# Running a depthwise convolution chunk by chunk on VectorE, with a mark for each chunk

## The chip, the cores and the metric

The kernel runs on one core of one Trainium2 chip. The metric is the device time of one execution in microseconds (us). The kernel before the change took 1326.59 us, the median of three runs (1323.63 to 1327.82).

The core's engines are named as the profile names them: PE is TensorE (matmuls; PEld is its weight load), DVE is VectorE, ACT is ScalarE, POOL is GpSimd, SP is SyncE, which issues every DMA here.

## The reference, cut to what matters

Two layers of a hybrid block work on 1024 latent tokens and 256 context tokens with 1024 channels. In each layer one input projection feeds three branches: a convolution module (256 channels), windowed attention with rotary tables (512) and a gated linear attention, GLA (256). Each branch is multiplied by a SiLU gate of its own, and one output projection joins them. The last layer needs no convolution, gate or output for the context tokens. The convolution module is:

```python
u = p['a_val'] * jax.nn.sigmoid(p['a_glu'])
u = lax.conv_general_dilated(u, conv_w[:, None, :], window_strides=(1,), padding=((15, 15),),
        feature_group_count=CONV_WIDTH) + conv_b          # depthwise, 31 taps along the tokens
mu, var = mean and variance of u over the 256 channels
u = (u - mu) * lax.rsqrt(var + NORM_EPS) * ln_w + ln_b
return jax.nn.silu(u) * jax.nn.silu(p['a_gate'])
```

## The kernel before, in words

**Layout.** Channels lie on the 128 partitions and tokens along the free dimension. The 256 convolution channels are two halves j = 0, 1. The 1280 tokens are three chunks, `CH`: chunk 0 is the 256 context tokens, chunks 1 and 2 are 512 latent tokens each. `col(t)` puts a gap of 15 columns between context and latents, so layer 0's whole token axis is 1280 + 15 = 1295 columns. The buffer `U[j]` holds the convolution's input with 15 zero columns at each end and in the gap. `mix` holds the three branches' results.

**The taps.** `conv_taps(l)` runs 31 taps for two halves on DVE. Each is one instruction over the whole axis, 1295 columns in layer 0 and 1024 in layer 1: the first tap is a `tensor_scalar` (input times weight plus bias), each other one a `scalar_tensor_tensor` that reads `U` shifted by s columns and the sum so far in `mix`, and writes the sum. These are the rows `mix<-U,small,mix` of the profile; both tensor inputs lie in SBUF. After the last one the mark `conv{l}` is set.

**What waits for the mark.** `ev_agate` takes the gate's projection out of PSUM (ACT `Tanh`, then one DVE instruction `U<-SM,ps`) and writes it over `U`, which the taps must have read by then. `conv_ln(l, c)` norms one chunk: PE transposes `mix` (rows `ps<-idr,mix`), DVE takes `BN_STATS`, PE transposes back, ACT and DVE apply swish and gate.

**What sets the order.** The program is a set of generators ("lanes") with priorities. A planner in the kernel keeps an estimated clock for each engine and asks the lanes, by priority, for their next instructions while it writes each engine's instructions in one fixed order. On the chip, each engine then runs its row in that order and waits where an operand is not ready. A lane can wait for a mark, a buffer, or an engine's estimated clock. The taps have the lowest priority of their stage (7) and are asked for with `yield self.idle("dve", 300)`: only when DVE's estimated queue reaches no more than 300 ns ahead. So they are put as filler between the DVE instructions of the other lanes.

**The stage.** `phase_a(l)` issues the projection groups in the order 0, 1 (the convolution's input), 10 (GLA values and decay), 8 (GLA queries and keys), 5, 3, 4 (attention keys, values, queries), 2 (the convolution's gate), 9, 6, 7 (other gates). `t_group` and `tok_group` issue the matmuls of a group. The taps start after group 1. The norm's lane is created behind the whole of group 2:

```python
            elif g == 2:
                yield from self.t_group(l, g, self.ev_agate(l), cx)
                def ln(): ...
                self.go(ln(), 3)
```

While the taps run, three other kinds of work go on. `gla_decay` makes the decays (`tensor_tensor_scan` on DVE). `gla_states` makes, for a chunk and a direction, e = last − b on DVE (`SM<-mix`), its exponential on ACT, its product with the keys on POOL (`SM<-SM,mix`), and PE's transposes of that product (`ps<-idr,SM`); later DVE adds up states (`mix<-mix,dec,ps`). `rope` turns keys and queries with five POOL instructions for each pair of token tiles: two `WR<-SM,SM`, one `SM<-SM,SM`, two `SM<-SM,WR`. `gla_out` makes the outputs of a token tile (`COPY_PREDICATED`, `TENSOR_REDUCE` and others on DVE). `split` cuts weights into two parts on ACT, DVE or POOL, whichever the planner thinks is free (`WS<-WR,WS`). `load_vz` issues the DMAs `SM<-vd`.

All instructions are issued through one helper, so every row has its line, L43.

Of the kernel before, what the change touches and what calls it, by code (L numbers as in the profile page):

```python
# [13 lines left out]
ALU = mybir.AluOpType  # L14
# [9 lines left out]
CH = [(0, 256), (256, 512), (768, 512)]  # L24


def col(t):
    return t if t < 256 else t + GAP
# [140 lines left out]
class Hybrid:  # L169
# [692 lines left out]
    def ev_agate(self, l):  # L862
        def ev(j, p, t0, n, c):
            nc = self.nc
            yield self.need("SM"), f"conv{l}"
            s = self.sm(512)
            t = s[:, 0:n]
            nc.scalar.activation(t, p, ACTF.Tanh, scale=0.5)
            yield
            nc.vector.scalar_tensor_tensor(self.U[j][:, col(t0):col(t0) + n], t, 1.0, p, op0=ALU.add, op1=ALU.mult)  # L870
            self.free(s)
            self.flag(f"ag{l}.{j}.{c}")
        return ev
# [71 lines left out]
                self.nc.vector.memset(self.U[j][:, a:a + n], 0.0)  # L945

    def conv_taps(self, l):
        nc = self.nc
        a, n = (0, 1295) if l == 0 else (271, 1024)
        for s in range(31):  # L950
            for j in range(2):
                yield self.idle("dve", 300)
                acc = self.mix(j, slice(a, a + n))
                src = self.U[j][:, a + s:a + s + n]
                if s == 0:
                    nc.vector.tensor_scalar(acc, src, self.p_conv_w(l, j, s), self.p_small(l, 62, j),
                                            op0=ALU.mult, op1=ALU.add)
                else:
                    nc.vector.scalar_tensor_tensor(acc, src, self.p_conv_w(l, j, s), acc, op0=ALU.mult, op1=ALU.add)
        self.flag(f"conv{l}")  # L960

    def conv_ln(self, l, c):
        nc = self.nc
# [620 lines left out]
    def phase_a(self, l):  # L1584
        cx = (0, 1) if l == 0 else ()
        self.units, self.pre, self.pcount = [], 0, 0
        self.conv_pad()
        if l:
            self.cap = dict(mm=2, tr=4, ac=2, md=2)
            self.evs = []  # L1590
        else:
            yield from self.t_start()
        first = (2, 0) if l == 0 else (1, 2, 0)
        for g in GROUPS[:-1]:
            if g == 10:
                self.cap = dict(mm=3, tr=2, ac=2, md=1)
                self.go(self.gla(l), 2)
                yield from self.vlr_group(l)
            elif g == 0 and l:
                yield from self.t_group(l, 0, self.ev_glu, cx, (1,), last=False)  # L1600
                yield from self.t_group(l, 1, self.ev_val, cx, (1,), last=False)
                yield from self.t_group(l, 0, self.ev_glu, cx, (2,))
            elif g == 0:
                yield from self.t_group(l, g, self.ev_glu, cx, first)
            elif g == 1:
                yield from self.t_group(l, g, self.ev_val, cx, (2,) if l else first)
                evs = tuple(self.evs)

                def conv():
                    yield evs  # L1610
                    yield from self.conv_taps(l)
                self.go(conv(), 7)
            elif g == 8:
                yield from self.t_group(l, g, self.ev_qk(l), (0, 1) if l == 0 else (1,))
                self.flag(f"qk{l}")
            elif g == 5:
                yield from self.tok_group(l, g, self.ev_qk_b(l, "kv", self.kd, 2))
            elif g in (3, 4):
                yield from self.tok_group(l, g, self.ev_qk_b(l, f"q{g - 3}", self.qd[:, :, (g - 3) * 256:(g - 2) * 256], 4), l == 0)
            elif g == 2:  # L1620
                yield from self.t_group(l, g, self.ev_agate(l), cx)

                def ln():
                    for c in range(1 if l else 0, 3):
                        yield from self.conv_ln(l, c)
                self.go(ln(), 3)
            elif g == 9:
                yield from self.t_group(l, g, self.ev_mgate(l, 6), cx)
            else:
                self.cap.update(mm=2, tr=CAPB[0], ac=CAPB[1])  # L1630
                self.cap["md"] = 0 if l else MDC
                if l:
                    self.flag(f"hcfree{l}")
                for n, (p, c) in enumerate(B_GATE):
                    if n == ATTN:
                        self.attn = self.go(self.attn_start(l), 1)
                    yield from self.t_group(l, p, self.ev_gate(l, 2 * p - 10), cx, order=(c,), last=all(x[0] != p for x in B_GATE[n + 1:]))
                    if n == MODG:
                        self.flag("mods")
                    if (p, c) == (7, 1):  # L1640
                        self.h1_keep()
                    if p == 7:
                        self.flag({0: f"hcfree{l}", 1: f"h1out{l}", 2: f"h2out{l}"}[c])
# [212 lines left out]
```

## Time and profile before

| | |
|---|---|
| median of three runs | 1326.59 us |
| the profiled execution | 1323.65 us, its span 1321.9 us |
| PE | 1254.0 us busy, 95% of the span |
| DVE | 838.4 us, 63% |
| ACT | 561.2 us, 42% |
| POOL | 452.9 us, 34% |
| mean granted PE clock | 0.991 |

The span is the time from the first to the last instruction. Rows of the timeline give start, duration, engine, operation, output tile <- input tiles, shape and a count; in brackets stands how long the engine had been idle before and what it waited for. Several instructions of a kind that follow each other are one row. PEclk is the granted clock of PE, 1.00 being full speed.

### The profile page before, as it was taken

To read this page: it belongs to the slowest core of one execution; us is meant where nothing else is said; L and a number is where in the kernel's file an instruction comes from. 1 tells how busy PE (TensorE), PEld (TensorE's weight loads), DVE (VectorE), ACT (ScalarE), POOL (GpSimd) and SP (SyncE) were. 2 spreads that over 40 slices of the span, in tenths; PEclk is the share of its full clock that TensorE was granted. 3 is DMA by queue.
4 is the path that set the end of the run, shared out by engine and by line. 5 is a ranking of instruction groups with operands and counts; after the bars stand their busy time and mean duration, and the time that the engine had idled before them with its cause. 6 is when DMAs were issued, how large, how long until landed. Compare 5 with 4: busy or idle time off the path is not lost.

```text
span 1321.9 us, 24553 instructions
## 1 busy us (share of the span) xinstructions
PE 1254.0 (95%) x9518; PEld 1066.9 (81%) x9518; DVE 838.4 (63%) x1571; ACT 561.2 (42%) x1280; POOL 452.9 (34%) x609
## 2 busy tenths in 40 slices
PE   6999988999999999899999899988999999999997
PEld 3668988898887777687899879977888888788897
DVE  5745897884364463465354676898954656766554
ACT  3721341235332565466541561441245246665531
POOL 1410045674122342444230241055571334344410
PEclk9999989999999999999999999999999999999999
DMA  9453113222014323342132541114231112231012
GB/s 330 151 154 105 48 39 85 70 69 85 25 33 131 112 77 100 96 129 89 49 113 88 156 164 57 49 41 108 71 91 37 55 46 81 73 93 50 33 65 81
DMA packets 113237, 116.49 MB, mean 88 GB/s; under 512 B 38464, under 2 KB 81760, under 8 KB 113120
## 3 DMA queue, kind: packets, MB, share of 16 engines
q1 hardware_dynamic: 113120, 114.92, 28.5%
q8 instruction: 75, 1.23, 0.4%
q14 instruction: 42, 0.34, 0.1%
HBM read 95.47 MB, written 19.42 MB: 87 GB/s over the span
## 4 chain that ended last, share of the span: by engine, by line
PE 69%; DVE 8%; POOL 6%; DMA 6%; issue 5%; ACT 4%; SPq 1%; POOLq 0%; DVEq 0%; ACTq 0%
PE ps L43 69%; POOL SM L43 4%; DVE SM L43 3%; ACT SM L43 2%; DVE mix L43 2%; DMA WR<-in_w_out_dram 2%; DVE H L43 2%; DMA WR<-in_w_mod_dram 2%; POOL WR L43 1%; DMA WR<-in_w_in_dram 1%; DVE WS L43 1%; SPq L43 1%; DMA HC<-in_w_mod_dram 1%; ACT H L43 1%; ACT L43 0%
## 5 line engine op out<-in xcount | busy, mean ns | idle before, releaser
L43 PE MATMUL ps<-H,WS 128*128 128x512 f32 x1344 | 339.7, 400 | 2.9 <-DVE stat L43 1.4
L43 PEld LDWEIGHTS ps<-H,WS 128*128 128x128 f32 x1344 | 244.3, 189 | 63.8 <-issue 12.2
L43 PE MATMUL ps<-WS,H 128*128 128x256 f32 x1744 | 254.8, 291 | 0.0
L43 PEld LDWEIGHTS ps<-WS,H 128*128 128x128 f32 x1744 | 230.4, 195 | 10.0 <-issue 9.5
L43 ACT ACTIVATE SM<-ps 128x512 f32<-128x512 f32 (+2 forms) x164 | 82.7, 509 | 343.6 <-PE ps L43 289.3
L43 DVE SCALAR_TENSOR_TENSOR mix<-U,small,mix 128x1295 f32<-128x1295 f32 (+1 forms) x120 | 180.9, 1549 | 0.0
L43 PE MATMUL ps<-idr,SM 128*128 128x128 f32 (+1 forms) x1076 | 150.5, 273 | 26.2 <-POOL SM L43 16.4
L43 PEld LDWEIGHTS ps<-idr,SM 128*128 128x128 f32 (+1 forms) x1076 | 120.0, 142 | 56.0 <-POOL SM L43 22.0
L43 DVE CUSTOM_DVE_ANT_0 SM<-ps,SM,small 128x640 f32<-128x640 f32 (+2 forms) x128 | 102.7, 813 | 60.1 <-PE ps L43 53.5
L43 ACT ACTIVATE SM<-SM,stat 128x641 f32<-128x641 f32 (+2 forms) x144 | 110.7, 769 | 69.5 <-DVE stat L43 47.2
L43 POOL TENSOR_TENSOR tir<-tir,mhalf 128x1 f32<-128x1 f32 (+2 forms) x55 | 47.3, 863 | 199.2 <-DVE tir L43 192.3
L43 POOL TENSOR_TENSOR SM<-SM,SM 128x128 fp32r<-128x128 f32 (+3 forms) x59 | 60.9, 1041 | 158.7 <-ACT SM L43 107.9
L43 PE MATMUL ps<-H,H 128*128 128x256 f32 x592 | 99.0, 287 | 3.7 <-DVE H L43 2.0
L43 ACT ACTIVATE H<-ps 128x512 f32<-128x512 f32 (+1 forms) x129 | 72.7, 596 | 65.2 <-PE ps L43 63.7
L43 POOL TENSOR_SCALAR SM<-SM,tir 128x640 f32<-128x640 f32 (+2 forms) x90 | 75.8, 855 | 44.3 <-DVE tir L43 29.7
L43 PEld LDWEIGHTS ps<-H,H 128*128 128x128 f32 x592 | 83.8, 189 | 5.5 <-DVE H L43 2.2
L43 ACT ACTIVATE SM<-SM 32x128 f32<-32x128 f32 (+3 forms) x194 | 70.3, 369 | 38.3 <-DVE SM L43 30.0
L43 PE MATMUL ps<-SM,SM 128*32 128x128 f32 (+4 forms) x764 | 79.0, 285 | 5.9 <-DMA SM<-vd 3.1
L43 PE MATMUL ps<-H 128*64 128x256 f32 x548 | 72.3, 388 | 0.7 <-ACT ps L43 0.3
L43 POOL TENSOR_TENSOR SM<-SM,WR 128x256 f32<-128x256 f32 (+2 forms) x60 | 61.8, 1036 | 20.0 <-DVE SM L43 13.8
L43 DVE TENSOR_TENSOR WS<-WR,WS 128x512 fp32r<-128x512 f32 x66 | 60.7, 932 | 5.2 <-ACT WS L43 3.6
L43 PEld LDWEIGHTS ps<-SM,SM 128*64 128x64 f32 (+2 forms) x764 | 45.4, 127 | 20.0 <-ACT SM L43 6.1
(151 smaller groups left out, 1989.8 us busy)
## 6 DMA issues: line engine op xcount, KB each, us to landing
WR<-in_w_in_dram SPq DMA_DIRECT2D x80, 256.0 KB, 3.7
WR<-in_w_mod_dram SPq DMA_DIRECT2D x64, 256.0 KB, 3.2
WR<-in_w_out_dram SPq DMA_DIRECT2D x32, 256.0 KB, 3.5
SM<-vd SPq DMA_DIRECT2D x116, 64.0 KB, 2.4
x<-SM SPq DMA_DIRECT2D x20, 256.0 KB, 2.5
SM<-x SPq DMA_DIRECT2D x20, 256.0 KB, 4.3
qd<-SM SPq DMA_DIRECT2D x18, 256.0 KB, 2.2
mix<-in_x_dram SPq DMA_DIRECT2D x8, 512.0 KB, 8.3
```

Source lines behind the costliest of these rows:

```text
L43: r = getattr(self._e, op)(*a, **k)
```

## The change

The convolution is run chunk by chunk: all 31 taps of both halves for chunk 0 (layer 0 only), then for chunk 1, then for chunk 2. A tap takes 256 or 512 columns in place of 1295 or 1024. After each chunk its mark `conv{l}.{c}` is set; the gate of that chunk waits for this mark alone, and so does the norm of that chunk.

```diff
     def ev_agate(self, l):
         def ev(j, p, t0, n, c):
             nc = self.nc
-            yield self.need("SM"), f"conv{l}"
+            yield self.need("SM"), f"conv{l}.{c}"
...
     def conv_taps(self, l):
-        nc = self.nc
-        a, n = (0, 1295) if l == 0 else (271, 1024)
-        for s in range(31):
-            for j in range(2):
-                yield self.idle("dve", 300)
-                acc = self.mix(j, slice(a, a + n))
-                src = self.U[j][:, a + s:a + s + n]
...
-        self.flag(f"conv{l}")
+
+        nc = self.nc
+        for c in range(1 if l else 0, 3):
+            a, n = col(CH[c][0]), CH[c][1]
+            for s in range(31):
+                for j in range(2):
+                    yield self.idle("dve", 300)
+                    acc = self.mix(j, slice(a, a + n))
+                    src = self.U[j][:, a + s:a + s + n]
...
+            self.flag(f"conv{l}.{c}")
...
                 def ln():
                     for c in range(1 if l else 0, 3):
+                        yield f"conv{l}.{c}"
                         yield from self.conv_ln(l, c)
```

The number of taps on DVE goes from 62 to 186 in layer 0 and from 62 to 124 in layer 1. The planner sees other estimated times and writes the rows in another order, within the two stages that hold the taps and for some way behind them.

First place: DVE in layer 0, about the second pair of GLA states. Before:

```order
L43 SCALAR_TENSOR_TENSOR mix_223_1356<-mix_223_1356,dec,ps_71 128x64 x4
L43 TENSOR_TENSOR SM_269_1764<-mix_223_1356 128x512
L43 SCALAR_TENSOR_TENSOR mix<-U,small,mix 128x1295 x6
L43 SCALAR_TENSOR_TENSOR mix_223_1356<-mix_223_1356,dec,ps_70 128x64 x8
L43 TENSOR_TENSOR SM_277_1930<-mix_223_1356 128x512
```

The same piece of DVE's row now:

```order
L43 SCALAR_TENSOR_TENSOR mix_223_1398<-mix_223_1398,dec,ps_71 128x64 x4
L43 TENSOR_TENSOR SM_269_1827<-mix_223_1398 128x512
L43 SCALAR_TENSOR_TENSOR mix<-U,small,mix 128x512 x14
L43 SCALAR_TENSOR_TENSOR mix_223_1398<-mix_223_1398,dec,ps_69 128x64 x8
L43 TENSOR_TENSOR SM_277_2000<-mix_223_1398 128x512
```

Six taps of 1295 columns have become fourteen of 512 at the same place; nothing else moved there. In layer 1 the piece that answers to it holds eight taps of 1024 columns before and fourteen of 512 now.

Second place: POOL in layer 0 at the same time, one rope and the product that PE's transposes wait for. Before:

```order
L43 TENSOR_TENSOR SM_267_1744<-SM_267_1744,mix 128x512
L43 TENSOR_TENSOR WR_273_1794<-SM_272_1793,SM_1_65 128x2x2x32 x2
L43 TENSOR_TENSOR SM_272_1793<-SM_272_1793,SM_1_65 128x2x128
L43 TENSOR_TENSOR SM_272_1793<-SM_272_1793,WR_273_1794 128x2x2x32 x2
L43 TENSOR_TENSOR SM_269_1764<-SM_269_1764,mix 128x512
```

Now:

```order
L43 TENSOR_TENSOR SM_267_1802<-SM_267_1802,mix 128x512
L43 TENSOR_TENSOR WR_273_1857<-SM_272_1856,SM_1_65 128x2x2x32 x2
L43 TENSOR_TENSOR SM_272_1856<-SM_272_1856,SM_1_65 128x2x128
L43 TENSOR_TENSOR SM_272_1856<-SM_272_1856,WR_273_1857 128x2x2x32 x2
L43 TENSOR_TENSOR SM_269_1827<-SM_269_1827,mix 128x512
```

Nothing moved here: the product still stands behind the whole rope.

Third place: DVE in layer 0 at the end of the convolution, where gate and norm follow (now; `U<-SM,ps` is the gate, `BN_STATS` the first row of the norm):

```order
L43 SCALAR_TENSOR_TENSOR mix<-U,small,mix 128x512 x4
L43 SCALAR_TENSOR_TENSOR U<-SM_369_3471,ps_66 128x512
L43 TENSOR_REDUCE tir<-SM_365_3348 128x4
L43 TENSOR_SCALAR tir<-tir 128x4
L43 SCALAR_TENSOR_TENSOR mix<-U,small,mix 128x512 x2
L43 TENSOR_TENSOR SM_365_3348<-ps_71,tir 128x256
L43 SCALAR_TENSOR_TENSOR mix<-U,small,mix 128x512 x5
L43 SCALAR_TENSOR_TENSOR U<-SM_371_3531,ps_67 128x512
```

Before, the last tap stood 14 rows ahead of the first gate row; now the gate rows of chunk 1 stand among the taps of chunk 2. The norm's first row stands behind the last tap of all in both kernels (by 45 rows before, by 8 now), and the norm's first transposes are row 865 of PE before and row 867 now.

More of the change, by code (lines that the diff above doesn't have):

```diff
@@ L948, in conv_taps @@
         nc = self.nc
-        a, n = (0, 1295) if l == 0 else (271, 1024)
-        for s in range(31):
-            for j in range(2):
-                yield self.idle("dve", 300)
-                acc = self.mix(j, slice(a, a + n))
-                src = self.U[j][:, a + s:a + s + n]
[L955 to L959, printed above, removed]
-        self.flag(f"conv{l}")
+        for c in range(1 if l else 0, 3):
[5 more added lines that the diff above has]
+                    src = self.U[j][:, a + s:a + s + n]
+                    if s == 0:
+                        nc.vector.tensor_scalar(acc, src, self.p_conv_w(l, j, s), self.p_small(l, 62, j),
+                                                op0=ALU.mult, op1=ALU.add)
+                    else:
+                        nc.vector.scalar_tensor_tensor(acc, src, self.p_conv_w(l, j, s), acc, op0=ALU.mult, op1=ALU.add)
+            self.flag(f"conv{l}.{c}")
     def conv_ln(self, l, c):
```

## The prediction

> **What bounds the kernel now.** I read the page first, then stretches, then the timelines of PE, POOL and DVE about PE's idle gaps.
>
> ```profile
> span 1321.9 us, 24553 instructions
> PE 1254.0 (95%) x9518; PEld 1066.9 (81%) x9518; DVE 838.4 (63%) x1571; ACT 561.2 (42%) x1280; POOL 452.9 (34%) x609
> PEclk9999989999999999999999999999999999999999
> ```
>
> PE is busy 95% of the span, so an edit that leaves PE's work alone can win at most its gaps and the time at a lower clock. The change touches the stages with the taps and what follows them:
>
> ```profile
> 175.00:300.00 125.00, 114.38 (x1084) 104.69 (x1083) 107.67 (x133) 35.81 (x95) 77.53 (x70) 0.96 0.27 69
> 875.00:950.00 75.00, 65.96 (x594) 57.66 (x595) 67.93 (x87) 16.10 (x41) 46.08 (x42) 0.95 0.36 94
> 302.00:400.00 98.00, 97.93 (x776) 83.09 (x773) 48.97 (x105) 38.53 (x103) 28.63 (x29) 1.00 0.18 51
> 962.00:1050.00 88.00, 88.00 (x692) 73.27 (x691) 42.38 (x89) 36.24 (x100) 32.00 (x34) 1.00 0.19 53
> ```
>
> Columns: length, then busy time of PE, PEld, DVE, ACT, POOL, then PE's clock. Among the taps PE is idle 10.6 us of 125 in layer 0 and 9.0 of 75 in layer 1, and its clock is 0.96 and 0.95. Just behind the taps, where gate and norm stand, PE is full. So the prize lies among the taps, and none behind them.
>
> ```profile
> 185.96 0.69 PE L43 MATMUL ps<-idr,SM 128*128 128x128 f32 x2 [3.59 <-POOL SM L43]
> ...
> 208.74 1.11 PE L43 MATMUL ps<-idr,SM 128*128 128x128 f32 x4 [3.65 <-POOL SM L43]
> 209.51 2.81 PE L43 MATMUL ps<-WS,H 128*128 128x256 f32 x12
> ...
> 212.83 1.69 PE L43 MATMUL ps<-WS,H 128*128 128x256 f32 x12
> ...
> 235.54 0.43 PE L43 MATMUL ps<-SM,SM 128*32 128x128 f32 x8 [1.07 <-DMA SM<-vd]
> 235.90 1.69 PE L43 MATMUL ps<-WS,H 128*128 128x256 f32 x12
> 876.61 0.44 PE L43 MATMUL ps<-idr,SM 128*128 128x128 f32 x2 [3.13 <-POOL SM L43]
> ...
> 897.60 0.66 PE L43 MATMUL ps<-idr,SM 128*128 128x128 f32 x4 [3.28 <-POOL SM L43]
> 898.02 2.80 PE L43 MATMUL ps<-WS,H 128*128 128x256 f32 x12
> ...
> 901.69 1.70 PE L43 MATMUL ps<-WS,H 128*128 128x256 f32 x12
> ```
>
> Four gaps stand out, two in each layer, all for POOL's product in `gla_states`. I call the first of each layer A (3.59 and 3.13 us) and the second B (3.65 and 3.28). Behind each B the same twelve matmuls take 2.81 and 2.80 us where they take 1.69 and 1.70 later: 1.1 us more, the lower clock. Behind the gap of 1.07 us they take 1.69: a short gap doesn't lower it.
>
> Why POOL is late at B, with DVE beside it:
>
> ```profile
> 198.67 2.21 POOL L43 TENSOR_TENSOR WR<-SM,SM 128x128 f32<-128x128 f32 x2 [1.83 <-ACT SM L43]
> 200.95 1.89 POOL L43 TENSOR_TENSOR SM<-SM,SM 128x256 f32<-128x256 f32 x1
> 202.92 3.28 POOL L43 TENSOR_TENSOR SM<-SM,WR 128x128 f32<-128x128 f32 x2
> 206.16 2.52 POOL L43 TENSOR_TENSOR SM<-SM,mix 128x512 f32<-128x512 f32 x1
> 209.09 0.87 POOL L43 TENSOR_TENSOR WR<-SM,SM 128x128 f32<-128x128 f32 x2 [0.40 <-ACT SM L43]
> 210.03 0.73 POOL L43 TENSOR_TENSOR SM<-SM,SM 128x256 f32<-128x256 f32 x1
> 210.84 0.87 POOL L43 TENSOR_TENSOR SM<-SM,WR 128x128 f32<-128x128 f32 x2
> ...
> 221.94 1.31 POOL L43 TENSOR_TENSOR SM<-SM,mix 128x512 f32<-128x512 f32 x1
> ...
> 887.92 2.96 POOL L43 TENSOR_TENSOR WR<-SM,SM 128x128 f32<-128x128 f32 x2 [0.51 <-ACT SM L43]
> ...
> 895.31 2.24 POOL L43 TENSOR_TENSOR SM<-SM,mix 128x512 f32<-128x512 f32 x1
> ```
> ```profile
> 121.99 1.56 DVE L43 SCALAR_TENSOR_TENSOR mix<-U,small,mix 128x1295 f32<-128x1295 f32 x1
> ...
> 123.93 5.99 DVE L43 SCALAR_TENSOR_TENSOR mix<-U,small,mix 128x1295 f32<-128x1295 f32 x4
> ...
> 178.61 5.53 DVE L43 SCALAR_TENSOR_TENSOR mix<-U,small,mix 128x1295 f32<-128x1295 f32 x3
> 184.06 0.75 DVE L43 TENSOR_TENSOR SM<-mix 128x256 f32<-128x256 f32 x2
> ...
> 197.31 10.26 DVE L43 SCALAR_TENSOR_TENSOR mix<-U,small,mix 128x1295 f32<-128x1295 f32 x6
> 213.03 2.50 DVE L43 SCALAR_TENSOR_TENSOR mix<-mix,dec,ps 128x64 f32<-128x64 f32 x8 [5.47 <-PE ps L43]
> ...
> 843.75 2.48 DVE L43 SCALAR_TENSOR_TENSOR mix<-U,small,mix 128x1024 f32<-128x1024 f32 x2
> 855.05 1.28 DVE L43 SCALAR_TENSOR_TENSOR mix<-U,small,mix 128x1024 f32<-128x1024 f32 x1
> 887.88 12.15 DVE L43 SCALAR_TENSOR_TENSOR mix<-U,small,mix 128x1024 f32<-128x1024 f32 x8
> ```
>
> From 198.67 to 208.69 POOL does one rope and the product in 10.0 us; the same six instructions take 0.87 + 0.73 + 0.87 + 1.31 = 3.8 where no tap runs (209.09 on, 221.94). The surplus of some 6.0 us, with 0.2 for seams, falls while DVE runs six taps back to back. They too stretch: four free taps step by (5.99 − 1.56) / 3 = 1.48 us, these six by 1.70. So POOL and the taps take turns, and each POOL instruction waits for about a tap. In layer 1 the six take 887.92 to 897.55 = 9.6 us, a surplus of 5.6; a free tap steps by 2.48 − 1.28 = 1.20, these eight by 1.55.
>
> **The change part by part.**
>
> *Length of a tap.* No row shows a tap of 512 or 256 columns. From the taps themselves, (1.48 − 1.20) / 271 gives 1.03 ns a column, so 0.67 and 0.41 us. The nearest rows with two SBUF inputs of 512 and 256 columns are
>
> ```profile
> L43 DVE SCALAR_TENSOR_TENSOR mix<-SM,U x10: 424/694/1671, 372.2 to 1094.8; 128x512 f32<-128x512 f32 x8, 128x256 f32<-128x256 f32 x2
> ```
>
> 0.694 and 0.424 us, less the overlap of 1.56 − 1.48 = 0.08: 0.61 and 0.34. I take 0.65 and 0.38, between them. One old tap of layer 0 becomes 0.38 + 2 × 0.65 = 1.68, 0.20 more; of layer 1, 0.10 more. With 62 each, DVE gets 12.4 + 6.2 = 19 us more (bounds 7 and 27).
>
> This is hidden as long as DVE has room: it is idle 17.3 of 125 us and 7.1 of 75 among the taps, and 49 of 98 and 46 of 88 behind them, where PE does not wait. The planner puts a tap in only where it sees DVE free, so the surplus runs on behind the stage (in the order the last taps of layer 0 stand among the first gate rows). Price 0; if the cover is gone it is a rival.
>
> [...]
>
> *Turns with POOL.* A wait is now for a tap of 0.65 in place of 1.48 or 1.20. In proportion, the surplus at B shrinks by 6.0 × 0.56 = 3.4 us and 5.6 × 0.46 = 2.6. (Were each wait exactly one tap: 5 × 0.83 = 4.2 and 6 × 0.55 = 3.3. Were POOL's turn not tied to the tap's length: 0.) I take the proportion. The order of POOL and of DVE there is unchanged, so the product ends 3.4 and 2.6 us earlier and the gaps shrink to 0.3 and 0.7 us. Such short gaps leave the clock, 1.1 us each. What is late next at B is the run of `mix<-mix,dec,ps`, for which DVE waited 5.47 us: room for a PE that comes earlier. B gives 4.5 + 3.7 = 8.2 us (0 to 9.1).
>
> [...]
>
> *Gaps A.* In layer 0, DVE runs three taps (178.61) before `SM<-mix` (184.06), whose result POOL multiplies for PE's transposes at 185.96; in the new order seven taps of 512 stand there (that piece of the order is not shown): 7 × 0.65 = 4.6 against 3 × 1.48 = 4.4, the turn with POOL alike. In layer 1:
>
> ```profile
> 872.59 0.74 DVE L43 TENSOR_TENSOR SM<-mix 128x256 f32<-128x256 f32 x2
> 874.07 1.44 POOL L43 TENSOR_TENSOR WS<-WR,WS 128x512 fp32r<-128x512 f32 x1
> 875.48 2.12 POOL L43 TENSOR_TENSOR SM<-SM,mix 128x256 f32<-128x256 f32 x2
> ```
>
> One tap ahead of `SM<-mix` becomes three of 512 (+0.7 us), but POOL is busy with a weight split until 875.51 anyway, 2.2 us after `SM<-mix` ends. Price 0 (−1 to +2).
>
> *The marks.* The norm's lane is still created behind group 2, and its rows stand behind the last tap as before. The gate waits for a shorter mark, but PE is full there. Price 0 (−1 to +1).
>
> *Other moves.* The small waits among the taps (1.07 us at 235.54 and a few of about 0.6) are met in another order. Price 0 (−2 to +3).
>
> Sum: −8.2 us on an execution of 1323.65 us. That lies 2.9 us below the median of the runs; carried over, 1326.59 − 8.2 = 1318 us.
>
> **The rivals.**
>
> *Another wait takes the place* (no change within 0.3%, some 4 us). PE freed at B meets the next supplier: ACT's copies that start each rope (the 1.83 us wait at 198.67), or DMAs of `vd` as at 235.54. For it: POOL waited for ACT ahead of this rope, so PE, ACT and POOL are nearly in step. Against: PE runs without a gap from 208.74 to 234.47 after B. It gives back half or more: 1323 to 1328.
>
> *DVE becomes the bound* (slower). Among the taps DVE has 17.3 and 7.1 us of room. If the fixed time of a tap is at its upper bound (27 us, some 60% of it within the two stretches = 16) and POOL's turns still hit as many taps, DVE's own links of the GLA chain (`SM<-mix`, state sums, outputs) come late and PE waits for them. It decides once more than about two thirds of the 24.4 us of room is used, since the room is not where it is needed. Price: 5 to 10 us, and no win at B: 1330 to 1336. Against: a waiting DVE instruction now has a shorter tap ahead of it.
>
> *The gaps A shrink too*, since POOL's subtraction ahead of the scans meets shorter taps: 3.6 + 3.1 us more, about 1311.
>
> **How the numbers follow.** My forecast (4 to 12 us won, 1314 to 1322.5) gets 0.57, the wait that takes its place 0.23, DVE as the bound 0.16, the larger win 0.04. 0.3% is about what a measurement can tell from no change: 1322.6 to 1330.6. The range of 1310 to 1330 takes in the first two cases and the last, and leaves out most of the third and the edges. Faster 0.60, same 0.24, slower 0.16.
>
> **What would show it.** Right: the two B gaps under 1 us with clock 1.00 behind them, POOL's rope and product at B in 6 to 7 us, taps of 512 stepping by about 0.65 free and 0.9 in turns, DVE's busy time up by about 19 us, the norm not earlier, A as before. Wrong: POOL at B still at 10 us; PE waiting for DVE in 175 to 300 or 875 to 950; a new gap behind B as long as the one that closed.

## The result, and the profile after

| | before | after |
| --- | --- | --- |
| median of 3 runs | 1326.59 us | 1337.28 us (1335.43 to 1337.76) |
| profiled execution | 1323.65 us, span 1321.9 | 1337.28 us, span 1335.5 |

The changed kernel is slower: the ratio is 1.0085, 95% interval 1.0058 to 1.0112. The forecast was 1318 us, a gain of 8.2 us. From the page of the changed kernel:

```profile
PE 1262.6 (95%) x9518; PEld 1071.0 (80%) x9518; DVE 872.4 (65%) x1749; ACT 562.9 (42%) x1283; POOL 448.0 (34%) x614
PEclk9999999999999999899999999999999999999999
```

PE runs the same 9518 matmuls and is busy 8.6 us longer. DVE has 34.0 us more, POOL 4.9 less.

To see where the time goes I cut both executions into three stages that hold the same number of PE's matmuls (the counts behind PE): layer 0 from its taps to behind its norm, the same of layer 1, and layer 1's rest, in which no tap runs. The columns are those of the stretches in the prediction; a stage's length less PE's busy time is PE's idle time. Before:

```profile
145.25:374.42 229.17, 218.48 (x1857) 191.84 (x1856) 169.30 (x231) 88.17 (x217) 101.34 (x93) 0.98 0.23 63
770.41:1059.85 289.44, 277.34 (x2076) 240.77 (x2075) 213.30 (x321) 100.26 (x234) 112.59 (x112) 0.99 0.24 66
1059.85:1312.76 252.91, 249.23 (x1916) 218.17 (x1916) 154.99 (x331) 128.00 (x275) 91.30 (x158) 1.00 0.21 66
```

After:

```profile
146.91:374.07 227.16, 216.84 (x1857) 190.01 (x1856) 189.02 (x318) 87.17 (x215) 93.06 (x92) 0.98 0.23 64
771.10:1060.75 289.65, 277.01 (x2076) 241.30 (x2075) 224.14 (x378) 100.07 (x233) 113.33 (x115) 0.99 0.24 66
1060.75:1325.77 265.02, 253.86 (x1916) 219.04 (x1916) 157.53 (x326) 130.32 (x279) 92.43 (x159) 0.99 0.20 63
```

With the taps the stages are 2.0 us shorter and 0.2 longer. The third, behind them, is 12.1 us longer: PE is idle 11.2 us in place of 3.7, and busy 4.6 us more for the same 1916 matmuls. The loss lies where the prediction had no step at all.

Among the taps the forecast turns did shrink. PE's gaps at the places that the prediction named, and what stands behind them (timeline of PE, after):

```profile
188.81 0.54 PE L43 MATMUL ps<-idr,SM 128*128 128x128 f32 x2 [3.26 <-POOL SM L43]
...
208.92 0.43 PE L43 MATMUL ps<-SM,SM 128*32 128x128 f32 x8 [0.59 <-DMA SM<-vd]
209.28 1.70 PE L43 MATMUL ps<-WS,H 128*128 128x256 f32 x12
...
225.50 0.43 PE L43 MATMUL ps<-SM,SM 128*32 128x128 f32 x8 [1.17 <-DMA SM<-vd]
247.82 0.65 PE L43 MATMUL ps<-SM,SM 128*64 128x256 f32 x4 [1.30 <-ACT SM L43]
249.11 0.65 PE L43 MATMUL ps<-SM,SM 128*64 128x256 f32 x4 [0.64 <-ACT SM L43]
250.40 1.11 PE L43 MATMUL ps<-SM,SM 128*64 128x256 f32 x4 [0.64 <-ACT SM L43]
...
878.21 0.44 PE L43 MATMUL ps<-idr,SM 128*128 128x128 f32 x2 [4.12 <-POOL SM L43]
...
898.13 0.43 PE L43 MATMUL ps<-SM,SM 128*32 128x128 f32 x8 [0.52 <-DMA SM<-vd]
...
985.79 0.33 PE L43 MATMUL ps<-SM,SM 128*64 128x64 f32 x2 [2.26 <-DVE SM L43]
```

Both B gaps (3.65 and 3.28 us) are gone, and the twelve matmuls behind the first take 1.70 us, with a granted clock of 1.00 there (209.28 to 210.98 us). But PE's idle time in layer 0's stage only goes from 10.7 to 10.3 us. PE's waits there, summed by what ended them (us in total, times, longest), before and after:

```profile
PE ps L43 <- POOL SM L43: 7.2, 2, 3.7
PE ps L43 <- ACT SM L43: 0.6, 1, 0.6
```
```profile
PE ps L43 <- POOL SM L43: 4.3, 3, 3.3
PE ps L43 <- ACT SM L43: 3.3, 5, 1.3
```

In place of B stand waits for ACT's copies in `gla_out` and, to a lesser part, for DMAs of `vd` (1.5 us before, 2.0 after): another wait takes the place, as the prediction's first rival said, though ACT's copies are others than those it named. The four matmuls at 250.40 take 1.11 us where the four before them take 0.65: the granted clock is 0.50 from 250.45 to 253.86 us, so the lower clock now falls there.

POOL at B (after), and a run of free taps of each length with the groups of all taps (before and after):

```profile
199.70 1.43 POOL L43 TENSOR_TENSOR WR<-SM,SM 128x128 f32<-128x128 f32 x2 [0.97 <-ACT SM L43]
201.21 1.07 POOL L43 TENSOR_TENSOR SM<-SM,SM 128x256 f32<-128x256 f32 x1
202.35 1.66 POOL L43 TENSOR_TENSOR SM<-SM,WR 128x128 f32<-128x128 f32 x2
203.97 1.74 POOL L43 TENSOR_TENSOR SM<-SM,mix 128x512 f32<-128x512 f32 x1
```
```profile
125.29 5.63 DVE L43 SCALAR_TENSOR_TENSOR mix<-U,small,mix 128x256 f32<-128x256 f32 x14
151.74 0.48 DVE L43 SCALAR_TENSOR_TENSOR mix<-U,small,mix 128x256 f32<-128x256 f32 x1
199.19 13.00 DVE L43 SCALAR_TENSOR_TENSOR mix<-U,small,mix 128x512 f32<-128x512 f32 x14
299.43 2.07 DVE L43 SCALAR_TENSOR_TENSOR mix<-U,small,mix 128x512 f32<-128x512 f32 x3
338.56 0.75 DVE L43 SCALAR_TENSOR_TENSOR mix<-U,small,mix 128x512 f32<-128x512 f32 x1
```
```profile
L43 DVE SCALAR_TENSOR_TENSOR mix<-U,small,mix 128x1295 f32<-128x1295 f32 x60 | 100.3, 1709 | 0.0
L43 DVE SCALAR_TENSOR_TENSOR mix<-U,small,mix 128x1024 f32<-128x1024 f32 x60 | 80.6, 1390 | 0.0
L43 DVE SCALAR_TENSOR_TENSOR mix<-U,small,mix 128x512 f32<-128x512 f32 x240 | 196.5, 873 | 0.0
L43 DVE SCALAR_TENSOR_TENSOR mix<-U,small,mix 128x256 f32<-128x256 f32 x60 | 24.3, 479 | 0.0
```

POOL's six instructions take 6.0 us in place of 10.0 (forecast 6.6). A free tap steps by (5.63 − 0.48) / 13 = 0.40 us and (2.07 − 0.75) / 2 = 0.66 us (forecast 0.38 and 0.65). In turns the fourteen step by 0.94.

### The profile page after: what moved, and what is told of

It is laid out like the page before. It is cut to its first block, busy times and chain, and to the rows that moved or that the text cites. A ratio compares the mean times of both kernels' runs of the same rounds, so it can differ in the third digit from the quotient of the medians.

```text
span 1335.5 us, 24744 instructions
## 1 busy us (share of the span) xinstructions
PE 1262.6 (95%) x9518; PEld 1071.0 (80%) x9518; DVE 872.4 (65%) x1749; ACT 562.9 (42%) x1283; POOL 448.0 (34%) x614
## 5 line engine op out<-in xcount | busy, mean ns | idle before, releaser
L43 PEld LDWEIGHTS ps<-WS,H 128*128 128x128 f32 x1744 | 229.3, 193 | 12.1 <-issue 11.2
L43 ACT ACTIVATE SM<-ps 128x512 f32<-128x512 f32 (+3 forms) x166 | 84.0, 509 | 326.6 <-PE ps L43 303.0
L43 DVE SCALAR_TENSOR_TENSOR mix<-U,small,mix 128x512 f32<-128x512 f32 (+1 forms) x300 | 220.9, 794 | 0.0
L43 POOL TENSOR_TENSOR SM<-SM,SM 128x128 fp32r<-128x128 f32 (+3 forms) x62 | 53.1, 866 | 164.4 <-ACT SM L43 114.4
L43 ACT ACTIVATE SM<-SM 32x128 f32<-32x128 f32 (+4 forms) x198 | 71.6, 368 | 56.4 <-DVE SM L43 47.9
L43 POOL TENSOR_TENSOR WS<-WR,WS 128x512 fp32r<-128x512 f32 x28 | 40.1, 1434 | 96.2 <-ACT WS L43 78.3
L43 POOL TENSOR_TENSOR SM<-SM,WR 128x256 f32<-128x256 f32 (+2 forms) x59 | 55.9, 953 | 23.2 <-DVE SM L43 11.7
```

Source lines behind the costliest of these rows:

```text
L43: r = getattr(self._e, op)(*a, **k)
```

## The experiments

Each is compared with the kernel before, run beside it on the same chip; what is won or lost is the ratio less 1, times that kernel's 1326 us. The time at which layer 0's stage begins differs by up to 5 us between executions, so stages are compared, not times from the start.

**One part alone, one part undone.** `same_order` issues the pieces of each tap back to back and tells the planner of one whole tap, so the rows of PE, ACT, POOL and SP stand as before:

```diff
+    o, x = self.mix(j, slice(b, b + m)), self.U[j][:, b + s:b + s + m]   # for each chunk, unseen by the planner
+    nc.vector._e.scalar_tensor_tensor(o, x, w, o, op0=ALU.mult, op1=ALU.add)
...
+    nc.issue("dve", "scalar_tensor_tensor", (acc, src, w, acc), {})      # the planner's whole tap
```

> Each tap is issued as three pieces (layer 0) or two (layer 1), back to back, where the kernel before issues one; the planner is told of one whole tap, so the order on PE, ACT, POOL and SP is that of the kernel before. Theory 'order' (shorter taps help POOL as forecast; the loss of the changed kernel comes from the other order in the second half of layer 1): the B gaps shrink, the lag behind layer 1's taps does not appear: 1316 to 1326 us, 0 to 10 us faster than before. Rival 'DVE load' (the taps' 40 us more of DVE time delay DVE's other work, and PE waits for it): 5 to 15 us slower than before, with PE waiting for DVE among the taps.

Measured: 1332.75 us, 1.0047 (1.0029 to 1.0066), slower by 6.2. Neither theory holds alone. The time lies in the range of 'DVE load'; the third stage is as before (252.43 us), as 'order' said, but layer 0's stage has grown to 233.85. POOL's six instructions at B take 5.5 us here (201.21 to 206.66), with POOL's rows in their old order, so the shorter taps alone let them end sooner. In the timeline of PE B is closed, but A is longer and there is a new gap; DVE's timeline shows what stands ahead of the second:

```profile
188.45 0.69 PE L43 MATMUL ps<-idr,SM 128*128 128x128 f32 x2 [6.37 <-POOL SM L43]
263.08 0.47 PE L43 MATMUL ps<-SM,SM 128*64 128x64 f32 x2 [4.18 <-DVE SM L43]
```
```profile
254.14 7.23 DVE L962 SCALAR_TENSOR_TENSOR mix<-U,small,mix 128x256 f32<-128x256 f32 x9
261.29 0.76 DVE L43 COPY_PREDICATED SM<-gmask,ps 128x256 f32<-128x256 uint8 x2
```

Nine pieces (three old taps) take 7.23 us, where the free steps above give an estimated 3 × (0.40 + 2 × 0.66) = 5.2, and the mask for which PE waits is queued behind them. Pieces that the planner doesn't count make DVE's own links late, as the rival said.

`layer0_only` and `layer1_only` cut the taps in one layer and leave the other whole, with its old order.

```diff
-        for c in range(1 if l else 0, 3):
-            a, n = col(CH[c][0]), CH[c][1]
+        whole = [(0, 1295)] if l == 0 else [(271, 1024)]
+        chunks = [(col(t), m) for t, m in CH[1 if l else 0:]]
+        first = 1 if l else 0
+        for c, (a, n) in enumerate(chunks if l == 0 else whole, first):   # l == 1 in layer1_only
...
```

> Chunk by chunk in layer 0 alone; layer 1 as before, with whole taps and its old order. Theory 'order': within 3 us of before, since the changed kernel's trace shows a gain of some 4 us at B and 3.3 us given back at 247 to 272 us. Rival 'DVE load': about half of the loss or more, 5 to 8 us slower, since layer 0 has 124 of the 180 new taps.

Measured: 1321.52 us, 0.9967 (0.9949 to 0.9984): 4.4 us faster, more than the theory gave. DVE's load is no loss there.

> Chunk by chunk in layer 1 alone; layer 0 as before. Theory 'order': 9 to 14 us slower than before, nearly the whole loss, and it arises behind 1060 us, where no tap runs. Rival 'DVE load': 2 to 6 us slower, and it arises among the taps (875 to 990 us).

Measured: 1339.39 us, 1.0108 (1.0081 to 1.0135), 14.3 us slower. The second stage takes 291.67 us (2.2 more), the third 267.07 (14.2 more). This is as much as the whole loss or more (0.3 us beyond the range of 'order'), and it arises behind the taps.

`one_mark` keeps the chunks but sets one mark a layer, and lets the norm go without one.

```diff
-            self.flag(f"conv{l}.{c}")
+        self.flag(f"conv{l}")
...
-                        yield f"conv{l}.{c}"
```

> The changed kernel with chunked taps, but with one mark a layer, set behind the last chunk, for the gate, and none for the norm, as before. Theory 'order' and rival 'DVE load': as the changed kernel within 3 us (1334 to 1340). Rival 'marks' (the gate and the norm of a chunk, let in by their own marks, crowd the engines): the loss is gone, 1322 to 1330.

Measured: 1340.87 us, 1.0114 (1.0085 to 1.0143). That is 0.9 us above the range for 'order', and far from the 1322 to 1330 of 'marks': the marks are not the cause.

**Two orders behind the taps.** Built with other margins in the conv lane, the kernels fall into two families: the last fifth of the rows of PE, DVE, ACT and POOL stands word for word either as before (the old tail) or as in the changed kernel (the new tail), with cut and with whole taps.

```diff
-                yield self.idle("dve", 300)
+                yield self.idle("dve", 200)    # whole taps: 200, 600; chunks: 600, 0
```

> The kernel before with whole taps and its marks; only the margin in the conv lane is 200 in place of 300 (the modelled free time of DVE ahead of which a tap may be put in). Built so, the last fifth of the rows of PE, DVE, ACT and POOL stands exactly as in the changed kernel (the 'new tail'), though no tap is cut. Theory 'tail' (the loss of some 13 us behind 1060 us belongs to that order, whichever taps led to it): 8 to 16 us slower than before, all of it behind 1060 us. Rival 'chunks' (the loss needs the shorter taps or the marks): within 4 us of before.

Measured: 1335.09 us, 1.0066 (1.0042 to 1.0089), 8.8 us slower.

> As the kernel before, whole taps, margin 600. It too is built with the new tail, and with another order among the taps than margin 200. Theory 'tail': 8 to 16 us slower than before, with the same loss behind 1060 us. Rival 'chunks': within 4 us of before.

Measured: 1341.05 us, 1.0113 (1.0091 to 1.0136), 15.0 us slower.

> The changed kernel, chunk by chunk with all its marks in both layers; only the margin is 600. Built so, the last fifth of the rows stands exactly as in the kernel before (the 'old tail'). Theory 'tail': the loss is gone and what the chunks win among the taps of both layers shows: 1314 to 1326 us, 0 to 12 us faster than before. Rival 'chunks': 1334 to 1340, as the changed kernel.

Measured: 1323.31 us, 0.9983 (0.9965 to 1.0000).

> The changed kernel with margin 0: the new tail again, with another order among the taps. Theory 'tail': 1332 to 1342 us, as the changed kernel. Rival 'margin' (the margin itself, not the tail, decides): different from the changed kernel by more than 5 us.

Measured: 1332.50 us, 1.0043 (1.0028 to 1.0057), just within what theory 'tail' allowed and close to what 'margin' asked for (by the ratios it is 5.6 us faster than the changed kernel). Its third stage is that of the new tail all the same; in the traces its layer 0 stage is 2.6 us shorter (224.57 us). The third stage of these four, in the same order:

```profile
1055.54:1320.47 264.93, 253.58 (x1916) 219.07 (x1916) 157.59 (x326) 130.37 (x279) 92.37 (x159) 0.99 0.20 63
```
```profile
1061.01:1328.77 267.76, 255.50 (x1918) 220.04 (x1917) 159.08 (x330) 130.49 (x279) 93.09 (x159) 0.99 0.20 63
```
```profile
1063.25:1315.47 252.22, 248.89 (x1916) 218.25 (x1916) 154.93 (x331) 128.14 (x275) 91.33 (x158) 1.00 0.21 66
```
```profile
1054.58:1320.04 265.46, 254.72 (x1916) 219.72 (x1916) 158.32 (x326) 130.33 (x280) 92.30 (x159) 0.99 0.20 63
```

Over all traces the old tail takes 252.2 to 252.9 us and the new one 264.9 to 267.8, whether the taps are cut or whole. That settles where the loss belongs: to the order of layer 1's second half, which small shifts of the taps tip one way or the other.

**What the cut itself is worth.** With the old tail in each, and margin 0 (or 200) in layer 0:

> Layer 0 chunk by chunk with margin 0, layer 1 with whole taps, margin 300 and the old tail. In the traces so far PE's idle time over the same matmuls of layer 0 is 10.1 to 11.4 us with cut and with whole taps alike (only the cut taps in the old order had more), and the length differs by the time at half clock. Theory 'clock' (the closed B gap reappears as other waits; what is won is half-clock time): PE's idle there again 10 to 11 us, 0 to 3.4 us at half clock in place of 10.2, so 3 to 6 us faster than before: 1320 to 1324. Rival 'gap' (the gap's time itself is won, as forecast): idle there down to 6 to 7 us and 6 to 9 us faster.

Measured: 1320.12 us, 0.9944 (0.9927 to 0.9961), 7.4 us faster (5.2 to 9.7): the lowest median of all.

> Whole taps in both layers and the old tail; only the margin of layer 0 is 200 in place of 300, so that its taps and PE's rows stand in another order there. Theory 'clock' (another order among the taps that leaves fewer stretches at half clock wins without any cut): 2 to 4 us faster than before, 1322.5 to 1325. Rival 'cut' (the gain of the kernels with cut taps needs the cut): within 1.5 us of before.

Measured: 1325.15 us, 0.9992 (0.9975 to 1.0009): another order without the cut wins nothing that shows. 'Cut' holds, but this is one order only, with another margin than the cut kernel's, and its interval reaches 3.3 us faster, into what 'clock' gave. That the gain needs the cut is likely, not shown. Layer 0's stage of the two:

```profile
147.25:372.72 225.47, 217.09 (x1857) 191.08 (x1856) 188.81 (x322) 86.96 (x214) 89.70 (x90) 0.98 0.24 64
```
```profile
144.05:372.43 228.38, 217.71 (x1857) 190.13 (x1856) 173.14 (x233) 88.47 (x217) 106.28 (x91) 0.99 0.24 63
```

PE's idle time there is 8.4 us with the cut and 10.7 without, POOL's busy time 89.70 against 106.28: part of the closed gap is kept, part comes back as other waits. So the run with the cut lies between its theories: its gain is what 'gap' gave, its idle time stands between 'clock' (10 to 11) and 'gap' (6 to 7). One trace is not exact here. The four traces with the cut and margin 0, all with the same order of matmuls in this stage, have 8.2 to 10.1 us of idle time, the five with whole taps 10.4 to 11.7.

> Both layers chunk by chunk, margin 0 in layer 0 and 500 in layer 1, which gives the old tail. Theory 'clock': layer 0 as in the run with layer 0 cut alone; in layer 1 idle among the taps again some 12 us, and its half-clock time (3.4 to 13.7 us in the traces so far) decides: 1317 to 1326. Rival 'gap': 1312 to 1318.

Measured: 1322.25 us, 0.9969 (0.9952 to 0.9987).

> As the run with 500, but margin 650 in layer 1: the old tail, another order among the taps of layer 1. Theory 'clock': 1317 to 1326. Rival 'gap': 1312 to 1318.

Measured: 1321.92 us, 0.9967 (0.9949 to 0.9986). Both times lie in the range of 'clock' and outside that of 'gap'. Cutting layer 1 as well, with the old tail, wins nothing over layer 0 alone (about 3 us the other way, with intervals that overlap), and PE's idle time in the second stage is 15.0 and 14.5 us, against 12.1 in the kernel before. In the run with 500 the B gap of layer 1 is gone too, and PE waits elsewhere (parts of its timeline):

```profile
926.96 0.43 PE L43 MATMUL ps<-SM,SM 128*32 128x128 f32 x8 [1.58 <-DMA SM<-vd]
940.26 0.65 PE L43 MATMUL ps<-SM,SM 128*64 128x256 f32 x4 [2.06 <-ACT SM L43]
...
967.66 0.65 PE L43 MATMUL ps<-SM,SM 128*64 128x256 f32 x4 [0.98 <-ACT SM L43]
...
972.76 0.33 PE L43 MATMUL ps<-SM,SM 128*64 128x64 f32 x2 [1.16 <-DVE SM L43]
```

**What costs the time in the new tail.** Its longest gap, in PE's timeline of the changed kernel, and POOL's work ahead of it:

```profile
1198.00 0.86 PE L43 MATMUL ps<-HC 128*128 128x256 f32 x6
1201.93 0.44 PE L43 MATMUL ps<-idr,SM 128*128 128x128 f32 x2 [3.07 <-POOL SM L43]
1202.71 2.37 PE L43 MATMUL ps<-idr,SM 128*128 128x128 f32 x10 [0.33 <-POOL SM L43]
```
```profile
1199.37 1.30 POOL L43 TENSOR_TENSOR H<-mix,H 128x512 fp32r<-128x512 f32 x1 [7.17 <-DVE H L43]
1200.65 2.00 POOL L43 TENSOR_SCALAR SM<-SM,tir 128x640 f32<-128x640 f32 x2
```

The same gap of 3.07 or 3.08 us stands in the traces of the five other kernels above with this tail; with the old one no gap in this stage reaches 1 us. Two runs keep the order and take POOL out of one link each (the planner is still told of POOL):

```diff
-                  ("pool", 150 + 2.1 * n, lambda: nc.gpsimd.tensor_tensor(o, a, b, op=ALU.subtract)))
+                  ("pool", 150 + 2.1 * n, lambda: self.sub_pool(o, a, b)))   # layer 1's output projection: on DVE
```

> The changed kernel with its new tail and the same rows on PE, ACT and SP; in layer 1 the three subtractions that split the input of the output projection (`H<-mix,H` and `SM<-mix,H`) and were put on POOL are issued on DVE, while the planner is still told of POOL. In the changed kernel POOL waits 7.17 us for one of them (1199.37 to 1200.67) with two scalings of attention rows queued behind it, for which PE waits 3.07 us (1201.93), and half clock follows. Theory 'head of line' (POOL's queue makes that gap): the gap falls below 1.5 us and the half clock behind it goes: 3 to 5 us faster than the changed kernel, 1332 to 1335 where that is 1337. Rival 'thin cover' (PE has too few independent rows there, so another supplier shows at once): within 1.5 us of the changed kernel.

Measured: 1337.28 us, 1.0090 (1.0072 to 1.0109).

```diff
-                  ("pool", 110 + 1.1 * n, lambda: nc.gpsimd.tensor_scalar(o, a, s, f, op0=ALU.mult, op1=ALU.mult)),
+                  ("pool", 110 + 1.1 * n, lambda: self.scale_pool(o, a, s, f)),   # layer 1's attention rows: on DVE
```

> The changed kernel with its new tail and the same rows on PE, ACT and SP; in layer 1 the scalings of the attention rows (`SM<-SM,tir`, 128x640 and 128x512) that were put on POOL are issued on DVE, while the planner is still told of POOL. Theory 'head of line': PE's waits for POOL behind 1060 us (0.45, 1.02, 3.07, 0.33 and 0.25 us) go, 4 to 8 us faster than the changed kernel: 1329 to 1333. Rival 'thin cover': the waits come back as waits for DVE, within 2 us of the changed kernel or slower.

Measured: 1338.61 us, 1.0089 (1.0065 to 1.0112). Neither wins. The gap is there in both, with another supplier's name:

```profile
1203.54 1.97 PE L43 MATMUL ps<-idr,SM 128*128 128x128 f32 x8 [3.67 <-DVE H L43]
```
```profile
1206.92 3.98 PE L43 MATMUL ps<-idr,SM 128*128 128x128 f32 x20 [3.89 <-DVE SM L399]
```

'Head of line' falls: POOL's queue alone doesn't make the gap. 'Thin cover' is left, with its forecast met, but it is not shown. Both runs put the work on DVE, whose rows in the changed kernel already follow each other from 1198.27 to 1209.97 us with no wait that the trace shows, so a DVE that is full at this point would give the same result.

The gap is 3.07 us of the 7.5 that PE is idle more in the new tail; the rest are gaps of about 1 us or less. Of the 4.6 us that PE is busy more, half clock accounts for at most 1.7: the changed kernel's clock record has 3.41 us of it there, from 1202.77 us on. The other 2.9 us were not traced to any instruction. Which single row of the plan tips it from one tail to the other was not found.

## Why the prediction was wrong

*The step that failed* is "Other moves", priced 0 (−2 to +3). It counted the small waits among the taps and stopped there; "PE is full behind them" was read from 302 to 400 and 962 to 1050 us. The planner's answer to new tap lengths reached some 335 us further (the last tap ends at 990.38 us, the third stage at 1325.77), to a stretch that holds no tap, and cost 12.1 us in the third stage. That is as much as the whole measured loss (1326.59 × 0.0085 = 11.3 us). No rival described it: the one that ended slower put its price among the taps.

*Turns with POOL:* right in place and near in size. POOL took 6.0 us at B in place of 10.0 where 6.6 was forecast (5.5 in `same_order`, with POOL's rows in their old order), and in both layers the gap went below 1 us. That each POOL instruction waits for about a tap was the author's estimate; the runs show only that POOL's time at B goes down with the taps' length. *What B is worth* was wrong in layer 1, and right in layer 0 by its size alone. The forecasts were −4.5 and −3.7 us; cutting layer 0 alone measured −4.4 (−6.8 to −2.1), layer 1 with the old tail nothing. The term counted a closed gap as won time, while in both layers PE met the next supplier: the `vd` DMAs, ACT's copies, and in layer 1 DVE's masks. That was the first rival. It can be read in the second stage: 289.44 us before, 289.65 after, idle 12.1 and 12.6 us. In layer 0 the agreement with −4.5 is luck as far as the traces tell. With the order of the changed kernel and of `layer0_only` the stage is 2.0 us shorter. Idle time gives 0.4 and 0.3 us of that in place of 3.4, and 3.41 us less of half clock (6.83 in place of 10.24) gives 1.7; PE's busy time there falls from 218.48 to 216.84 and 216.75 us. The two traced executions differ by 1.7 us in all (1321.98 and 1323.65), so the rest of the 4.4 us, a difference of medians, can't be placed with them. With margin 0 more of the gap is kept (idle 8.2 to 10.1 us).

*DVE's price:* forecast +19 us (7 to 27), measured 39.9 in the taps' groups (196.5 + 24.3 − 100.3 − 80.6; the first of each chunk aside). The upper bound of 27 us is 186 more taps at 0.145 us, which the free steps of 1.48 and 1.20 us leave beside 1.03 ns a column. The part that free taps show was well sized: 0.40 + 2 × 0.66 − 1.48 = 0.24 us an old tap in layer 0 and 0.12 in layer 1, times 62, some 22 us. Missing was that the taps' side of the turns doesn't shrink with them. Busy time divided by count stands 0.19 us (1295 columns) and 0.14 us (1024) above the free step before, 20 us in all, and 0.16 us above it for 240 taps of 512 after, 38 us: another 18, which makes 40 in all. So the free steps give 22 us, and the turns nearly double that.

*Hidden at price 0:* mostly so in layer 0. In layer 1 DVE's load shows as the new 2.26 us wait at 985.79, and `same_order` shows what it costs (6.2 us) if the planner doesn't make room for it. *Gaps A* at 0: 3.59 to 3.26, 3.13 to 4.12, within −1 to +2. *Marks* at 0: right.

## What to carry to other kernels

Where a planner or scheduler sets the order, a changed duration is a changed order for everything behind it, so compare the orders to their ends and give each stretch that differs a bound of its own, also far from the edit. Then hold the order fixed, or find builds with and without the edit that share it: here that parted a gain of 2 to 7 us from a loss of some 12 that whole taps can meet as well. A gap that closes is won only if the next supplier is early: count idle time over the whole stage, not at the gap.

## What the runs showed of the hardware

In the clock records of the kernel before and of the changed kernel the lower clock is half clock (0.50) in stretches of 3.41 or 6.83 us, all but the last of each, which is 5.89 and 8.46 us long and runs past the span's end. With the same order of matmuls on PE in the second stage, three executions had 6.8, 10.2 and 17.1 us of it (kernel before, `layer0_only`, `cut0_margin0`; clock and length of the last two beside the 0.99 and 289.44 us above):

```profile
768.00:1058.42 290.42, 278.21 (x2076) 241.81 (x2075) 211.19 (x320) 100.26 (x234) 110.57 (x111) 0.98 0.24 66
```
```profile
768.14:1060.26 292.12, 280.59 (x2076) 243.46 (x2075) 210.86 (x322) 100.30 (x234) 111.14 (x112) 0.97 0.24 66
```

So two executions can differ by 1 to 3 us in a stage that no edit touched, and only the medians tell such sizes.

In the changed kernel the clock record has a drop at 250.45 us. It follows waits of 1.30, 0.64 and 0.64 us with matmuls between them: of the 3.41 us ahead of it PE was idle some 2.1. So it came here without a single gap as long as A or B (3.13 to 3.65 us before).
